# Attention items by feature tile and query tile instead of by head, with one weight pair moved

## The chip, the cores and the metric

The kernel runs on one core of one Trainium2 chip. The metric is the device time of one execution in microseconds (us), as the median of several runs.

## What is computed

Two blocks run one after the other on 256 tokens of 1024 features: a first block (a mixer and a mixture of experts) and a second block of two layers (l = 0 and 1), each with a feed-forward network, an attention part and another feed-forward network. The change is in the attention part of the second block. Cut to what matters there (16 heads of 64 features; 6 window heads with a sink, 4 global heads, 6 neighbourhood heads with a bias; every head sees 256 tokens and 256 context tokens as keys):

```python
p = u @ w_in[l]
q_w, q_g, q_n = _split_q(p[..., :MIX_WIDTH_2])
k_w, v_w, k_g, v_g, k_n, v_n = _split_kv(p[..., MIX_WIDTH_2:])
...
y_w = _window_attn(q_w, k_w, v_w, ck_w, cv_w, sink_win[l])
y_g = _global_attn(q_g, k_g, v_g, ck_g, cv_g)
y_n = _neighbourhood_attn(q_n, k_n, v_n, ck_n, cv_n, rpb_nbr[l])
h = h + gm * (jnp.concatenate([y_w, y_g, y_n], axis=-1) @ w_out[l])
if not last:
    yc = jnp.concatenate([_ctx_attn(cq_w, ck_w, cv_w, sink_win[l]),
                          _ctx_attn(cq_g, ck_g, cv_g),
                          _ctx_attn(cq_n, ck_n, cv_n)], axis=-1)
    hc = hc + cgm * (yc @ w_out[l])
```

where each of these is softmax(q k^T / 8 + bias or mask) v over both kinds of keys.

## The kernel before

Activations lie as [128 features, block, 512 columns]: columns 0 to 255 (X in the code) are the tokens, 256 to 511 (C) the context. All large products run on TensorE (PE) with each operand split into a high and a low part (H and L), so every product is three matmuls. `mm` (line 352) makes the products of one weight tile (a "unit"). Before a unit can run, its raw weights are loaded by SP's queue into one of the tiles `raw`, ScalarE (ACT) casts the high part (`emit_hi`, line 257) and VectorE (DVE) subtracts the low part (`emit_lo`), into a pair of tiles from the list `hls`. That list holds four pairs of its own; other pairs are lent to it for a limited part of the program, from pools that are open then (`extra`) or from attention tiles that are not yet, or no longer, in use (in `mix`, `pt` and two pairs out of the value tiles).

The order of the work is set when the program is built. Main work (units) is emitted in turn; every 3000 columns `work` calls `tick`, which lets background generators take one step each. The attention is such a generator: `attention` is a pipeline over items, and in each step it emits, for the items p1, p2 and p3 of the steps before,

- `t_out(p2)`: the transposed probabilities go from PSUM to the tiles ptH (ACT, line 701) and ptL (DVE),
- `exps(p1)` (ACT, line 908) and `sums(p1)`: exponentials, the reciprocal of their sums (DVE), and the scaling of the first half of the probabilities by DVE and of the second by ACT (line 927),
- `scores` of the new item (PE, line 872) and `maxes` (DVE, which for items with a mask or bias also adds the tile `bias`; then `bias_load` loads the next bias by POOL's queue),
- `v_out(p3)`, `values(p2)` (PE, line 974), `transposes(p1)` (PE, line 942).

Each `yield` hands back to the main program. While units are there, a unit's matmuls (line 352, or line 830 for the values' projections) fill in between; I call this fill. Where the main program has nothing to run before the attention is through (`until` and `drain` in `mix`), the steps follow each other without fill.

A feature tile of 128 rows holds two heads of 64 features. Of items of kind "x" (tokens as queries) there are 16 in each layer, one for each head: i is the feature tile, r the head in it, so that all six score matmuls of an item (64 x 128 weights, 512 columns) read the rows of one half, 64 r to 64 r + 63, three for each of the two query tiles of 128 tokens. Its values are 12 matmuls of 256 columns. Items of kind "c" (context as queries, layer 0 alone, 8 of them) take both heads at once: twelve score matmuls of 256 columns, whose rows alternate between the two halves, and twelve value matmuls. After the attention, `us` holds the output projection: four units over the first five blocks of the features (they are the fill of the last items), then, after `drain(att)`, four over the last three blocks and four over all eight.

Of the kernel before, what the change touches and what calls it, by code (L numbers as in the profile page):

```python
# [32 lines left out]
FR, FH = 8, 0  # L33
# [34 lines left out]
class Free:  # L68
    """Tiles handed out in turn; some are lent, only to units before a limit."""
# [46 lines left out]


class Vector:
    """The vector engine, with a count of the time that its work takes."""
# [14 lines left out]
class Unit:  # L134
    """One weight tile's product: out += W^T rhs over nk blocks of the contraction."""
# [6 lines left out]
class Program:  # L142
# [37 lines left out]
    def warm(self, n):  # L180
        """Keeps the tensor engine's clock up over a wait: products that nobody reads."""
# [26 lines left out]
    def plan(self, mains, adas=(), at=lambda t: t, lead=0, rest=12):  # L208
        """Units in the order of their use, the ones of w_ada spread between the others."""
# [78 lines left out]
    def fill(self):  # L288
        """The parts of a fixed number of weight tiles ahead, and the modulations due by now."""
# [32 lines left out]
    def get_raw(self):  # L322
        """The next of the tiles that are used as they come."""
# [9 lines left out]
    def w(self, i, c):  # L333
        """The parts of a weight tile: the columns a to b of its block k of c."""
# [6 lines left out]
    def mm(self, u, cols, ks=None, start=True, stop=True, parts="HhL"):  # L341
        """parts: H and L are the weight's parts by the activation's first, h the first by its second."""
# [21 lines left out]
    def run_lead(self, us, cols):  # L364
        """Units whose products with the activation's first part go ahead of the others."""
# [37 lines left out]
    def rsqrt(self, ssq, n, scale, parts=None):  # L403
        """rs = (scale * ssq + eps)^-1/2."""
# [15 lines left out]
    def square_in(self, k, cols, src=None):  # L420
        """ssq += src^2, the running sum over the blocks of features; the last square waits."""
# [34 lines left out]
    def norm(self, cols, A, B=None, slow=False):  # L456
        """u = h * rs * A + B into the two parts of u; slowly, between other work, and with few banks."""
# [25 lines left out]
    def scaled(self, cols, A, B, bc, slow=0):  # L483
        """u = h * A * bc + B in two parts; the first part runs ahead of the second."""
# [51 lines left out]
    def ada_next(self):  # L536
        """One block of a modulation vector, for both streams: the rows of w_ada^T by silu(c)."""
# [24 lines left out]
    def silu_c(self, pool, limit):  # L562
        """silu of the two vectors that the modulations come from."""
# [24 lines left out]
    def swiglu(self, f, end):  # L588
        """Epilogues of a gate and an up unit: hid[f] = silu(gate) * up, in two parts."""
# [117 lines left out]
    def rope_tail(self, raw, H, L):  # L707
        """H + L = raw * cos + rot(raw) * sin; raw is [128, 256] of SBUF."""
# [104 lines left out]
    def v_units(self, name, ws, c0, width, per):  # L813
        """Values, token by token: v[:, tile, c0:c0 + width] = u^T W."""
# [29 lines left out]
    def bias_load(self, src):  # L844
        for j in range(2):
            self.nc.gpsimd.dma_start(self.bias[:, j, X], src[:, j, :])

    def attention(self, l, items):
        """Pipelined over the heads: each step has the scores of one, the transposes of the one
        before and the values of the one before that."""  # L850
# [6 lines left out]
        def scores(it):  # L857
            kind, i, r = it["k"], it["i"], it["r"]
# [16 lines left out]
        def maxes(it):  # L875
            """The maxima over the keys, with their sign turned."""
            kind, i, r = it["k"], it["i"], it["r"]
# [5 lines left out]
            for j in range(2):  # L883
# [3 lines left out]
                if it["masked"]:  # L887
                    self.v.tensor_tensor_reduce(out=pj, in0=sj, in1=self.bias[:, j, :], scale=-1.0,
# [1326 lines left out]
```

## Time and profile before

| | |
|---|---|
| median of 3 runs | 2054.43 us (2053.01 to 2055.33) |
| span of the profiled execution, first to last instruction | 2051.0 us |
| time of the profiled execution, by the median | 2054.43 us, so 3.4 us lie around the span |
| busy share of the span: PE, PE weight loads, DVE, ACT, POOL | 98%, 86%, 69%, 41%, 3% |
| the chain of waits that ended last, share of the span by engine | PE 80%, DVE 2%, ACT 2%; by line PE L352 70%, PE L872 2%, PE L974 2%, PE L942 2% |
| attention of layer 0, from the first scores to the end of the last values | 726.9 to 900.5 us |
| attention of layer 1 | 1705.7 to 1825.2 us |

The profile follows one execution. A matmul's duration in it includes the way through the array, so that matmuls overlap; what one costs is read from the distance of starts, or from the chain of waits, which counts each stretch of time once.

### The profile page before, as it was taken

What the parts mean: (1) busy time and instruction counts of PE and PEld (TensorE: products, weight loads), DVE (VectorE), ACT (ScalarE), POOL (GpSimd) and SP (SyncE); (2) the same over time, 40 slices, a digit from 0 to 9 for tenths busy, and PEclk for the clock granted to TensorE, in tenths of its full rate; (3) what the DMA queues carried; (4) which work ended last, traced back from release to release, by engine and by line L of the source; (5) the groups of instructions that cost most, each with busy time, mean ns of one, the idle gap of its engine ahead of it and who ended that gap; (6) DMA issues with size and microseconds to landing.
All of it is one profiled execution on the core that took longest, in us unless ns stands there. A gap on an engine that the chain in (4) does not pass through costs nothing.

```text
span 2051.0 us, 29852 instructions
## 1 busy us (share of the span) xinstructions
PE 2003.9 (98%) x11780; PEld 1757.0 (86%) x11780; DVE 1417.3 (69%) x2368; ACT 838.7 (41%) x1428; POOL 65.3 (3%) x87
## 2 busy tenths in 40 slices
PE   7989989999999999999999999999999999999998
PEld 7977769888888988789888888988888899889998
DVE  6888886888863756777886745788674366767554
ACT  5457653222222456764322222422222245655442
POOL 1200000000000100000000000000000011000000
PEclk9999999999999999999999999999999999999999
DMA  6669973565540311135655533366553122147551
GB/s 235 202 240 362 360 262 123 182 206 197 188 130 22 109 58 39 37 98 179 216 200 176 166 113 113 117 202 195 167 172 108 57 85 74 47 130 240 180 172 44
DMA packets 92596, 318.08 MB, mean 155 GB/s; under 512 B 11616, under 2 KB 14976, under 8 KB 92064
## 3 DMA queue, kind: packets, MB, share of 16 engines
q1 hardware_dynamic: 88496, 306.75, 45.2%
q0 software_dynamic: 2624, 9.08, 1.3%
q8 instruction: 94, 1.54, 0.3%
q14 instruction: 54, 0.44, 0.1%
q10 hardware_dynamic: 1328, 0.27, 0.1%
HBM read 315.01 MB, written 1.05 MB: 154 GB/s over the span
## 4 chain that ended last, share of the span: by engine, by line
PE 80%; DVE 2%; ACT 2%; issue 0%; DMA 0%; POOL 0%; POOLq 0%; DVEq 0%; ACTq 0%
PE bank L352 70%; PE bank L830 3%; PE bank L872 2%; PE bank L974 2%; PE bank L942 2%; DVE tmp L130 1%; ACT probs L908 1%; ACT ptH L701 0%; PE bank L453 0%; DVE uL L130 0%; DVE lo L130 0%; PE bank L449 0%; PE bank L796 0%; DMA raw<-in_w_ffn_up_dram 0%; DVE h L130 0%
## 5 line engine op out<-in xcount | busy, mean ns | idle before, releaser
L352 PE MATMUL bank<-uH,hi 128*128 128x512 f32 (+2 forms) x1128 | 384.1, 345 | 7.1 <-DVEq L1707 6.0
L352 PE MATMUL bank<-uH,lo 128*128 128x512 f32 (+2 forms) x1128 | 380.1, 341 | 0.6 <-DVE lo L130 0.6
L352 PE MATMUL bank<-uL,hi 128*128 128x512 f32 (+2 forms) x1128 | 364.8, 341 | 0.0
L130 DVE CUSTOM_DVE_ANT_0 tmp<-xraw,cs,vec 128x1024 bf16<-128x1024 f32 x192 | 245.9, 1282 | 3.4
L352 PEld LDWEIGHTS bank<-uH,hi 128*128 128x128 f32 x1128 | 217.6, 193 | 33.0 <-DVEq L1707 6.4
L352 PEld LDWEIGHTS bank<-uH,lo 128*128 128x128 f32 x1128 | 217.4, 193 | 23.7 <-DVE lo L130 0.8
L352 PEld LDWEIGHTS bank<-uL,hi 128*128 128x128 f32 x1128 | 207.9, 192 | 21.9
L352 PE MATMUL bank<-uH,xlo 128*128 128x512 f32 (+1 forms) x600 | 201.7, 338 | 0.0
L352 PE MATMUL bank<-uH,xhi 128*128 128x512 f32 (+1 forms) x600 | 201.7, 338 | 0.0
L130 DVE TENSOR_TENSOR lo<-xraw,hi 128x1024 fp32r<-128x1024 f32 (+1 forms) x138 | 164.6, 1200 | 50.6 <-ACT hi L257 50.2
L352 PE MATMUL bank<-uL,xhi 128*128 128x512 f32 (+1 forms) x600 | 198.1, 338 | 0.0
L604 ACT CAST hidH<-tmp 128x512 fp32r<-128x512 f32 (+1 forms) x97 | 51.6, 532 | 331.4 <-DVE tmp L130 331.3
L257 ACT CAST hi<-xraw 128x1024 fp32r<-128x1024 f32 (+1 forms) x138 | 141.1, 1030 | 102.9 <-PE bank L352 91.8
L130 DVE TENSOR_TENSOR lo<-raw,hi 128x1024 fp32r<-128x1024 f32 (+3 forms) x129 | 144.2, 1123 | 46.3 <-ACT hi L257 46.1
L130 DVE SCALAR_TENSOR_TENSOR h<-bank,modT,h 128x256 f32<-128x256 f32 x204 | 92.8, 480 | 112.1 <-PE bank L352 112.1
L352 PE MATMUL bank<-hidH,hi 128*128 128x256 f32 (+1 forms) x504 | 169.8, 337 | 0.0
L352 PE MATMUL bank<-hidL,hi 128*128 128x256 f32 (+1 forms) x504 | 169.1, 335 | 0.1
L352 PE MATMUL bank<-hidH,lo 128*128 128x256 f32 (+1 forms) x504 | 169.0, 335 | 0.0
L257 ACT CAST hi<-raw 128x1024 fp32r<-128x1024 f32 (+3 forms) x129 | 124.3, 968 | 60.8 <-PE bank L352 40.3
L595 ACT ACTIVATE tmp<-bank 128x512 f32<-128x512 f32 (+1 forms) x97 | 49.5, 510 | 232.3 <-PE bank L352 230.5
L130 DVE TENSOR_TENSOR tmp<-tmp,bank 128x512 f32<-128x512 f32 (+1 forms) x97 | 56.0, 577 | 122.9 <-PE bank L352 122.0
L130 DVE CUSTOM_DVE_ANT_0 tmp<-raw,cs,vec 128x1024 bf16<-128x1024 f32 x96 | 123.5, 1287 | 5.7 <-DVEq L1707 3.9
(408 smaller groups left out, 4227.9 us busy)
## 6 DMA issues: line engine op xcount, KB each, us to landing
xraw<-in_w_ada_dram SPq DMA_DIRECT2D x96, 512.0 KB, 3.4
xraw<-in_w_ffn_gate_dram SPq DMA_DIRECT2D x51, 512.0 KB, 3.4
xraw<-in_w_ffn_up_dram SPq DMA_DIRECT2D x51, 512.0 KB, 3.7
raw<-in_w_ada_dram SPq DMA_DIRECT2D x48, 512.0 KB, 4.3
xraw<-in_w_expert_gu_dram SPq DMA_DIRECT2D x43, 512.0 KB, 5.7
raw<-in_w_ffn_up_dram SPq DMA_DIRECT2D x37, 512.0 KB, 3.8
raw<-in_w_ffn_gate_dram SPq DMA_DIRECT2D x37, 512.0 KB, 4.3
xraw<-in_w_ffn_down_dram SPq DMA_DIRECT2D x32, 512.0 KB, 4.0
```

The lines of the kernel that those rows point to most:

```text
L130: return f(*args, **kw)
L257: self.nc.scalar.copy(hi, form(self.raw_of[i][0][:, :n], hi))
L352: nc.tensor.matmul(o, a(k), b[:, k, cols], start=start and k == ks[0] and j == 0, stop=stop and k == ks[-1] and j == len(prods) - 1, skip_ ...
L595: nc.scalar.activation(t[:, :cols.stop - cols.start], u.bank[:, cols], AF.Silu)
L604: nc.scalar.copy(H, tt)
L830: nc.tensor.matmul(b, x[:, kk, tok], y(k), start=first, stop=a == ws - 1 and k == per - 1 and j == 2, skip_group_check=True)
L872: nc.tensor.matmul(it["S"][j][:, o], a[rows, i, q], b[rows, kt, kk], start=n == 0 and o.start == 0, stop=n == 2, skip_group_check=True)
L908: nc.scalar.activation(it["P"][:, j, o], src[:, o], AF.Exp, scale=-1.0 if it["masked"] else 1.0, bias=st[:, c:c + 1], accum_out=st[:, 4 + ...
L942: nc.tensor.transpose(b[:, o * P:(o + 1) * P], src, self.ident)
L974: nc.tensor.matmul(b[:n, X], a[:, k + dk, v0:v0 + n], p[:, k, :], start=j == 0 and k == ks[0], stop=j == 2 and k == ks[-1], skip_group_che ...
```

## The change

An x item is now a feature tile and a query tile t (0 or 1) and holds both heads of the feature tile. Its six score matmuls are of the same shapes, but alternate between the rows 0 to 63 and 64 to 127. The transposed probabilities of the two heads go to two pairs `pts` instead of one pair `pt`, 128 columns (one query tile) at a time; so the values of a feature tile, 24 matmuls, are emitted together behind the second query tile, where 12 were behind each head. The bias is loaded for two heads and one query tile at a time, as two loads of the same size. Beside the second pair, `hls` keeps three pairs of its own instead of four. In the pools around the mixes a fifth pair is lent instead (in the first block's pool one instead of none, in the next one instead of none), and in the mixes' own ends four pairs instead of three; what is one less is the number of pairs while the attention runs. The change also drops comments.

```diff
-FR, FH = 8, 0
+FR, FH = 8, 1
...
-            kind, i, r = it["k"], it["i"], it["r"]
+            kind, i, t = it["k"], it["i"], it["t"]
...
             if kind == "x":
-                subs = [[(j, slice(0, 512), slice(j * P, (j + 1) * P), XC, r)] for j in range(2)]
+                subs = [(slice(0, 512), slice(t * P, (t + 1) * P), XC)]
             else:
-                subs = [[(j, slice(256 * a, 256 * a + 256), slice(256 + a * P, 256 + (a + 1) * P), C, j)
-                         for j in range(2)] for a in range(2)]
-            for sub in subs:
+                subs = [(slice(256 * a, 256 * a + 256), slice(256 + a * P, 256 + (a + 1) * P), C) for a in range(2)]
+            for o, q, kk in subs:
                 for n, (a, b) in enumerate(((self.hidH, self.kH), (self.hidH, self.kL), (self.hidL, self.kH))):
-                    for j, o, q, kk, rr in sub:
-                        rows = slice(64 * rr, 64 * rr + 64)
+                    for j in range(2):
+                        rows = slice(64 * j, 64 * j + 64)
...
         def values(it):
-            PH, PL = (t.rearrange("p (k q) -> p k q", q=256) for t in self.pt)
             if it["k"] == "x":
-                subs = [(r, range(4), 0)]
+                subs = [(1, range(4), 0), (0, range(4), 0)]
...
-            if p2:
+            if p2 and p2["t"] == 1:
                 yield from values(p2)
                 yield
...
-                for r in (1, 0):
-                    it = dict(k="x", i=i, r=r, need=need(i))
+                for t in range(2):
+                    it = dict(k="x", i=i, t=t, need=need(i))
...
-            self.hls = Free([(t(f"hi{i}", [P, 1024], F32R), t(f"lo{i}", [P, 1024], F32R)) for i in range(4)])
+            self.hls = Free([(t(f"hi{i}", [P, 1024], F32R), t(f"lo{i}", [P, 1024], F32R)) for i in range(3)])
...
-            def extra(fx, limit, n=4, hl=4):
+            def extra(fx, limit, n=4, hl=5):
...
-                    self.pt = (t("ptH", [P, 1024], F32R), t("ptL", [P, 1024], F32R))
+                    self.pts = [(t(f"ptH{j}", [P, 1024], F32R), t(f"ptL{j}", [P, 1024], F32R)) for j in range(2)]
...
-                extra(self.b1, limit0, n=2, hl=0)
+                extra(self.b1, limit0, n=2, hl=1)
```

How the order of instructions moves is shown at three places. In the rows, numbers behind a name are those of a buffer. First PE, layer 0, the score matmuls of one x item in the stretch without fill; the two banks are the two query tiles before, the two heads now. Before:

```order
L872 MATMUL bank_65<-kH,hidH 128x512
L872 MATMUL bank_65<-kL,hidH 128x512
L872 MATMUL bank_65<-kH,hidL 128x512
L872 MATMUL bank_69<-kH,hidH 128x512
L872 MATMUL bank_69<-kL,hidH 128x512
L872 MATMUL bank_69<-kH,hidL 128x512
```

Now:

```order
L873 MATMUL bank_67<-kH,hidH 128x512
L873 MATMUL bank_63<-kH,hidH 128x512
L873 MATMUL bank_67<-kL,hidH 128x512
L873 MATMUL bank_63<-kL,hidH 128x512
L873 MATMUL bank_67<-kH,hidL 128x512
L873 MATMUL bank_63<-kH,hidL 128x512
```

The same six matmuls now change bank, and with it the half of the rows, at each one.

Second PE, layer 1, in the stretch without fill: one step of the pipeline before (scores, twelve values, transposes).

```order
L872 MATMUL bank_69<-kH,hidH 128x512
L872 MATMUL bank_69<-kL,hidH 128x512
L872 MATMUL bank_69<-kH,hidL 128x512
L974 MATMUL bank_63<-ptH,vH 128x256 x4
L974 MATMUL bank_63<-ptH,vL 128x256 x4
L974 MATMUL bank_63<-ptL,vH 128x256 x4
L942 MATMUL bank_67<-ident,probs_13147 128x128 x4
L942 MATMUL bank_68<-ident,probs_13147 128x128 x4
```

Now, from the end of one item's scores to the end of the next one's, and on to the values:

```order
L873 MATMUL bank_66<-kH,hidL 128x512
L944 MATMUL bank_70<-ident,probs_13153 128x128 x4
L944 MATMUL bank_67<-ident,probs_13153 128x128 x4
L873 MATMUL bank_65<-kH,hidH 128x512
L873 MATMUL bank_63<-kH,hidH 128x512
L873 MATMUL bank_65<-kL,hidH 128x512
L873 MATMUL bank_63<-kL,hidH 128x512
L873 MATMUL bank_65<-kH,hidL 128x512
L873 MATMUL bank_63<-kH,hidL 128x512
L974 MATMUL bank_69<-ptH_13156,vH 128x256 x4
L974 MATMUL bank_69<-ptH_13156,vL 128x256 x4
L974 MATMUL bank_69<-ptL_13157,vH 128x256 x4
```

One step has no values at all, the next has 24 (the twelve shown, and twelve from the other pair behind them). Steps of the two kinds take turns.

Third ACT, at the end of layer 1's attention: the last copies of transposes and values, then squares of the new h (L426, L429) and the casts of the weights of the output projection (L257; `ptH` and `vH` serve as weight tiles there). Before:

```order
L701 CAST hidH<-bank_67 128x256
L426 ACTIVATE ssq<-h 128x256
L257 CAST ptH<-raw_86 128x1024
L429 ACTIVATE tmp_97<-h 128x256
L257 CAST vH<-raw_87 128x1024
L429 ACTIVATE tmp_99<-h 128x256
```

Now:

```order
L701 CAST hidH<-bank_66 128x256
L426 ACTIVATE ssq<-h 128x256
L257 CAST ptH_13154<-raw_85 128x384
L429 ACTIVATE tmp_95<-h 128x256
L257 CAST ptH_13156<-raw_86 128x1024
L429 ACTIVATE tmp_97<-h 128x256
```

Four of the units after the attention have 384 columns of weights. All four of them were cast before the attention ended; now the last of the four is cast behind it, and the ones of 1024 columns one place later.

## Rows read from the trace of the kernel before

**Rows 1.** The page, part 1: TensorE's busy time, share of the span, instructions.

```profile
PE 2003.9 (98%) x11780; PEld 1757.0 (86%) x11780; DVE 1417.3 (69%) x2368; ACT 838.7 (41%) x1428; POOL 65.3 (3%) x87
```

**Rows 2.** Windows over both attentions: stretch, length, busy us, clock, DMA.

```profile
core 0: us, PE busy (x) PEld busy (x) DVE busy (x) ACT busy (x) POOL busy (x), PEclk, DMA share, GB/s
726.90:822.30 95.40, 94.60 (x577) 79.37 (x576) 58.10 (x134) 55.08 (x145) 7.49 (x5) 1.00 0.15 48
822.30:854.10 31.80, 30.79 (x213) 25.19 (x213) 25.66 (x57) 26.63 (x69) 2.14 (x4) 1.00 0.08 24
854.10:880.00 25.90, 25.90 (x140) 20.67 (x139) 16.00 (x40) 11.90 (x28) 3.22 (x6) 1.00 0.27 79
880.00:900.50 20.50, 16.94 (x138) 13.83 (x137) 15.25 (x34) 16.76 (x49) 0.00 (x0) 1.00 0.08 27
1705.70:1775.60 69.90, 69.90 (x473) 62.68 (x472) 47.62 (x109) 42.23 (x98) 6.54 (x5) 1.00 0.22 65
1775.60:1798.80 23.20, 23.20 (x149) 19.00 (x149) 18.41 (x41) 17.95 (x41) 2.15 (x4) 1.00 0.13 36
1798.80:1825.20 26.40, 24.72 (x180) 21.75 (x179) 18.54 (x45) 16.68 (x38) 3.22 (x6) 1.00 0.31 98
```

**Rows 3.** The chain in order of time: start, us, what it waited through, instructions.

```profile
804.57 0.90 PE bank L872 x12
...
808.48 1.39 PE bank L352 x6
809.87 0.87 PE bank L942 x8
...
830.54 1.59 PE bank L872 x6
...
1721.13 1.44 PE bank L352 x12
```

**Rows 4.** Timeline of PE without fill, layer 0: start, us, what, idle before.

```profile
827.98 0.74 PE L974 MATMUL bank<-ptH,vH 128*128 128x256 f32 x4
...
829.50 1.04 PE L942 MATMUL bank<-ident,probs 128*128 128x128 f32 x8
...
832.06 0.68 PE L974 MATMUL bank<-ptH,vH 128*64 128x256 f32 x4
...
833.49 1.03 PE L942 MATMUL bank<-ident,probs 128*128 128x128 f32 x8
...
837.32 1.09 PE L942 MATMUL bank<-ident,probs 128*128 128x128 f32 x8 [0.27 <-DVE probs L130]
...
841.58 1.14 PE L942 MATMUL bank<-ident,probs 128*128 128x128 f32 x8 [0.72 <-DVE probs L130]
...
880.04 1.03 PE L942 MATMUL bank<-ident,probs 128*128 128x128 f32 x8
...
883.94 1.09 PE L942 MATMUL bank<-ident,probs 128*128 128x128 f32 x8 [0.34 <-DVE probs L130]
```

**Rows 5.** Timeline of ACT behind the transposes at 829.50.

```profile
830.14 1.07 ACT L701 CAST ptH<-bank 128x512 fp32r<-128x512 f32 x2 [0.43 <-PE bank L942]
...
832.80 0.73 ACT L927 ACTIVATE probs<-probs,sm 128x512 f32<-128x512 f32 x1 [0.23 <-DVE sm L130]
```

**Rows 6.** Timelines at the end of layer 1's attention: PE, ACT, DVE.

```profile
1825.22 0.28 PE L352 MATMUL bank<-hidH,hi 128*128 128x256 f32 x1
...
1827.69 1.03 ACT L257 CAST ptH<-raw 128x1024 fp32r<-128x1024 f32 x1
...
1828.75 1.23 DVE L130 TENSOR_TENSOR ptL<-raw,ptH 128x1024 fp32r<-128x1024 f32 x1 [0.35 <-ACT ptH L257]
```

**Rows 7.** Windows at a low and at the full granted clock.

```profile
1848.00:1850.00 2.00, 2.00 (x11) 2.00 (x10) 2.00 (x6) 2.00 (x7) 0.00 (x0) 0.50 0.72 287
1852.00:1854.00 2.00, 2.00 (x19) 2.00 (x18) 2.00 (x4) 1.98 (x2) 0.00 (x0) 1.00 0.00 0
890.00:901.00 11.00, 8.52 (x59) 6.60 (x57) 7.20 (x17) 8.67 (x30) 0.00 (x0) 1.00 0.01 1
```

More of the change, by code (lines that the diff above doesn't have):

```diff
@@ L842, in v_units, with bias_load @@
         self.have.add(name)
-    def bias_load(self, src):
-        for j in range(2):
-            self.nc.gpsimd.dma_start(self.bias[:, j, X], src[:, j, :])
+    def bias_load(self, srcs):
+        for j, src in enumerate(srcs):
+            self.nc.gpsimd.dma_start(self.bias[:, j, X], src)
     def attention(self, l, items):
@@ L875, in maxes @@
         def maxes(it):
-            kind, i, r = it["k"], it["i"], it["r"]
+            kind, i = it["k"], it["i"]
             it["P"] = self.probs.get()
@@ L887, in maxes @@
                 if it["masked"]:
-                    self.v.tensor_tensor_reduce(out=pj, in0=sj, in1=self.bias[:, j, :], scale=-1.0,
+                    bias = self.bias[:, it["t"] if i < 3 else j, :]
+                    self.v.tensor_tensor_reduce(out=pj, in0=sj, in1=bias, scale=-1.0,
                                                    scalar=nsk if it["sink"] else 3.0e38, op0=OP.add, op1=OP.min,
@@ L898, in head @@
         def head(it, j):
-            return 6 * l + it["i"] + 3 * (it["r"] if it["k"] == "x" else j)
+            return 6 * l + it["i"] + 3 * j
         def exps(it):
@@ L957, in values @@
         def values(it):
-            i, r = it["i"], it["r"]
+            i = it["i"]
             v0 = 0 if i < 3 else 128 if i < 5 else 256 + 128 * (i - 5)
-            PH, PL = (t.rearrange("p (k q) -> p k q", q=256) for t in self.pt)
             if it["k"] == "x":
-                subs = [(r, range(4), 0)]
+                subs = [(1, range(4), 0), (0, range(4), 0)]
             else:
                 subs = [(1, range(2, 4), 0), (0, range(2), 2)]
-            if it["k"] == "c" or r == 1:
-                self.vbank = yield from self.take(self.banks)
-            b = it["V"] = self.vbank
+            b = it["V"] = yield from self.take(self.banks)
             for rr, ks, dk in subs:
                 n = 64 * (rr + 1)
+                PH, PL = (t.rearrange("p (k q) -> p k q", q=256) for t in self.pts[rr if it["k"] == "x" else 0])
                 for j, (a, p) in enumerate(((self.vH, PH), (self.vL, PH), (self.vH, PL))):
@@ L1001, in attention @@
                 maxes(it)
-                if it.get("next") is not None:
+                if "next" in it:
                     self.bias_load(it["next"])
                 yield
-            if p3 and (p3["k"] == "c" or p3["r"] == 0):
+            if p3 and p3["t"] == 1:
                 v_out(p3)
-            if p2:
+            if p2 and p2["t"] == 1:
                 yield from values(p2)
@@ L1020, in att_items @@
             for i in grp:
-                for r in (1, 0):
-                    it = dict(k="x", i=i, r=r, need=need(i))
-                    n = 2 * (i - 5) + 1 - r
-                    if i == 2 and r == 0:
-                        it["next"] = self.I["bias"][l, 1]
-                    elif 0 <= n < 5:
-                        it["next"] = self.I["bias"][l, (n + 1) ^ 1]
+                for t in range(2):
+                    it = dict(k="x", i=i, t=t, need=need(i))
+                    n = 2 * (i - 5) + t if i > 4 else -1 if (i, t) == (2, 1) else 9
+                    if n < 5:
+                        a, nt = (n + 1) // 2, (n + 1) % 2
+                        it["next"] = [self.I["bias"][l, 2 * a + r, :, nt, :] for r in range(2)]
                     out.append(it)
@@ L1030, in att_items @@
                 for i in grp:
-                    out.append(dict(k="c", i=i, r=0, need=need(i)))
+                    out.append(dict(k="c", i=i, t=1, need=need(i)))
         return out
@@ L1037, in mix @@
         self.have = set()
-        self.bias_load(self.I["mask"])
+        self.bias_load([self.I["mask"][:, j, :] for j in range(2)])
         def qk(i):
@@ L1078, in mix @@
         f = lambda v: v.rearrange("p a c -> p (a c)")
-        self.hls.lend([self.pt] + [(f(self.vH)[:, 1024 * a:1024 * a + 1024], f(self.vL)[:, 1024 * a:1024 * a + 1024])
-                                   for a in range(2)], self.mix_end[l])
+        self.hls.lend(self.pts + [(f(self.vH)[:, 1024 * a:1024 * a + 1024], f(self.vL)[:, 1024 * a:1024 * a + 1024])
+                                  for a in range(2)], self.mix_end[l])
         if both:
```

8 lines of the change are left out of this document (4 added, 4 removed).

## The prediction

> **What bounds the kernel now.** Read the page first: PE is busy 98% of the span [rows 1], so time is won where PE's work gets shorter, and only there. Then the windows over the two attentions [rows 2]: seven stretches, 293 of 2051 us, cut where fill (matmuls of units between the steps) begins and ends. Stretches 1, 3 and 5 have fill; 2 and 6 have none, 4 none, and 7 has fill for its first half. In 1, 3, 5 and 6 PE hardly idles; in 2 and 4 it idles 1.0 and 3.6 us. Then the chain in order of time, for what a group costs on PE [rows 3]: six score matmuls of an x item take 1.59 us, twelve of half the columns in a c item, which alternate between the halves of the rows, 0.90. Both stream 3072 columns. That pair of rows is the price of the first part of the change, read before it is made. Last the timelines where there is no fill [rows 4, 5], for what a step costs when PE is not the bound.
>
> There, a step runs from transposes to transposes. At 829.50 to 833.49 PE takes 3.99 us: transposes 0.87, scores 1.59, values from 832.06 to 833.49 1.43, and 0.10 between groups [rows 3, 4]. But right behind it, where the scores were the cheap kind, the step from 833.49 to 837.32 took 3.83 and PE sat idle 0.27 before its transposes [rows 4]. That is a second chain, through other engines: ACT begins to copy 0.64 us after the transposes begin, copies for about 1 us, makes the exponentials, and DVE and ACT scale at 3.30 [rows 5]; half a microsecond later the next transposes may start. This chain has 3.83 us for an x item without a mask, 3.90 for one with a bias (880.04 to 883.94) and 4.26 for a c item (837.32 to 841.58) [rows 4]. It is just hidden now: 3.99 against 3.83. Scores are not in it.
>
> **The change part by part.** *Scores.* I price an x item's scores at 0.90 instead of 1.59, 0.69 less. Bounds: no overlap (1.59) and the c row (0.90); I take the c row, since shapes of 64 rows, banks and alternation are the same, and only the columns per matmul differ. 32 items would give 22 us.
>
> *Values.* Their 24 matmuls cost 1.52 (827.98 to 829.50) and 1.43 [rows 4] as before, 2.95. But steps now come in two kinds: A without values, B with all 24. With fill that is nothing. Without fill, A has 0.87 + 0.90 = 1.8 us of PE work and takes the chain's 3.83; B has 0.87 + 0.90 + 2.95 + 0.10 = 4.8, above the chain. A pair then costs 8.6 where two steps cost 8.0: the cheap scores gain nothing there, and the uneven values lose 0.6. An A step also has one yield less, so three pieces of fill where there were four; the attention runs ahead of its fill a little, which the sums below take from the order of PE's instructions.
>
> *Layer 0* [rows 2]. Stretch 1 (95.4): up to the last fill there are now eight x scores instead of seven, 12 more value matmuls and 3 fewer of fill (half of 1.39 [rows 3]): 8 x 0.90 - 7 x 1.59 + 1.42 - 0.69 = -3.2. Stretch 2 (31.8): the steps are now A, B, A, B and three with no or twelve values, which the chain sets: 3.83 + 4.8 + 3.83 + 4.8 + 4.26 + 3.90 + 3.90, and 0.87 to the fill: 30.2, so -1.6. Stretch 3 (25.9): three scores at -0.69, 12 more values, one group of transposes less: -2.07 + 1.42 - 0.87 = -1.5. Stretch 4 (20.5): only c items are scored; one B step of 4.8 takes the place of 4.26: +0.5. Together -5.8.
>
> *Layer 1.* Stretch 5 (69.9): seven scores -4.8, 12 more values +1.4, 9 fewer fill matmuls (9/12 of 1.44 [rows 3]) -1.1: -4.5. Stretch 6 (23.2): scores and the rest of the fill 2.0, then A, B, A, B and one A with a bias: 2.0 + 3.83 + 4.8 + 3.83 + 4.8 + 3.90 + 0.87 = 24.0, so +0.8. Stretch 7 (26.4): until the fill ends, 9.6 us up to the transposes (24 + 12 + 12 fill matmuls at 0.12, scores 0.90, values 2.95); then A with a bias 3.9, B 4.8, and the last transposes 3.9 later; 1.7 for their copies (0.64 + 1.07 [rows 5]) and 2.95 for the last values: 26.9, so +0.5. Together -3.2.
>
> *One pair less.* While units of 24 matmuls run, a freed pair is refilled in a cast of 1.03 and a subtraction of 1.23 [rows 6] while two others are used up: hidden, at no cost; without that cover 2.3 a unit. At the end of layer 1's attention it is not: the three pairs hold units of nine matmuls of 0.12, 1.08 us each. The fourth is cast behind the first square, which ends 2.47 us after the fill begins (1825.22, 1827.69 [rows 6]), and with both parts at 3/8 of the rows' durations is there at 3.4 at the earliest instead of 3.24; the fifth then at 3.4 + 1.03 + 1.23 = 5.7, where PE wants it at 4.5. About 1.3 us, with bounds 0 (DVE and ACT find a gap) and 3.5 (the raw load behind it, whose tile is freed later, is late too, and the norm's small DVE step now stands behind a subtraction that waits for that load). Layer 0's units there have twice the columns: nothing.
>
> *Bias loads, pools.* Same number, size and queue for the bias, one load each per head and step; its tile is freed after the maxima as before. In the pools the pairs lent grow by the one that the list lost. I cost both at 0; the cover is the main work around them. Without it, a pair that comes free late at a change of pools would cost up to 2.3 us, a cast and a subtraction; one that is free early wins nothing, since PE doesn't wait now.
>
> **Sum:** -5.8 - 3.2 + 1.3 = -7.7. The durations are those of one execution of span 2051.0, 3.4 below the median of 2054.43; the part around the span stays. 2054.43 - 7.7 = 2046.7; I say **2047**.
>
> **Rivals.** *1, everything is won:* PE sets the unfilled steps too, as it does now in stretch 6. 32 x 0.69 = 22 less: 2032.4. For it: no idle time of PE in stretch 6; against: the step of 3.83 with cheap scores, where PE did wait [rows 4]. With half of it, 13 less, 2041.
>
> *2, the chain binds beside fill as well:* a filled A step has 0.87 + 0.90 + 3 x 1.39 = 5.9 us on PE against 3.83 plus a weight cast of 1.03 and the copies of q and k on the same ACT. If half of the 19 filled scores' gain goes so, 6.5 of it is lost: 2053. Against: ACT and DVE are busy 58% to 68% in stretches 1 and 5 [rows 2]. The Trainium skill, "TensorEngine Tiling (Array Packing)", PSUM Bottleneck, speaks for it: packing speeds up the matmuls, not the copies out of PSUM, which may then be the bottleneck. By that rule alone the scores would gain nothing anywhere; the unfilled steps agree with it, the filled ones of stretches 1 and 5 so far do not.
>
> *3, slower, by the clock:* PE would idle about 2 us in every A step without fill. At the end of layer 1, where PE has only the norm's few small matmuls and waits for other engines between them, the granted clock fell to 0.50 (1.2 instead of 2.4 GHz), and then 11 matmuls started in 2 us instead of 19 [rows 7]. If it fell in stretches 2, 6 and 7, their five B steps would go from 4.8 to 4.8 x 19/11 = 8.3, and 2047 would become 2047 + 17.5 = 2064.5; two such steps turn the sign. Against: at 890 to 901 PE idles 2.5 of 11 us, and the clock is 1.00 [rows 7].
>
> *4, the scores don't overlap at 512 columns:* the price stays 1.59. Then the gain of the 19 filled scores (13.1) is gone, and four B steps and the unfilled scores at the head of stretch 6 cost 0.69 more each: 2046.7 + 13.1 + 3.5 = 2063.3.
>
> **How the numbers follow.** A measurement tells 0.2%, 4.1 us, from no change. Forecast (4 to 11 us less) 0.58; rival 1, all or half, 0.10; rival 2 and other losses of the weights that leave 0 to 4 us, 0.21; rival 3 0.05; rival 4 0.06. So faster 0.68, same 0.21, slower 0.11. The range, 8 in 10: from rival 1's half, 2041, to rival 2 with the end of layer 1 at 3.5 instead of 1.3, 2055. It leaves out most of rival 1 and all of 3 and 4.
>
> **What would show it.** Chain: x scores at 0.9 instead of 1.59. Timeline without fill: transposes 3.8 and 4.8 apart in turn, and PE idle 2 us before every second group, waiting for DVE or ACT on the probabilities. Stretch 1 near 92, stretch 5 near 65.5, stretches 6 and 7 no shorter. At the end of layer 1, a wait of PE for a subtraction behind the fourth unit. I am wrong if the unfilled steps all take 3.4 (rival 1), if PE waits for ACT inside the filled stretches (rival 2), if the clock falls below 1.00 there (rival 3), or if the scores stay at 1.6 (rival 4).

## The result, and the profile after

The change made the kernel slower: 2069.94 us (median of 4 runs, 2069.21 to 2073.69) against 2054.44 in runs on the same chip, ratio 1.0083, 95% interval 1.0070 to 1.0095. The forecast was 2047 with a range of 2041 to 2055; it missed by 23 us, on the other side of zero. The profiled execution after has a span of 2067.5 us, 16.5 more than before.

PE's part of the page says that it worked less and waited more. It is busy 7.3 us less than before [rows 1], in a span that is 16.5 longer:

```profile
PE 1996.6 (97%) x11780; PEld 1749.6 (85%) x11780; DVE 1415.4 (68%) x2368; ACT 838.6 (41%) x1428; POOL 64.8 (3%) x87
```

The windows over the same seven stretches, columns as in [rows 2], put the loss in the attentions: 308.1 us instead of 293.1, so 15.0 of the 16.5.

```profile
728.00:826.20 98.20, 95.10 (x594) 78.70 (x594) 60.43 (x140) 56.17 (x148) 6.92 (x5) 0.98 0.15 48
826.20:861.80 35.60, 27.61 (x194) 22.45 (x193) 24.48 (x55) 26.30 (x67) 2.32 (x5) 0.90 0.08 21
861.80:886.20 24.40, 24.40 (x144) 19.75 (x143) 15.72 (x40) 11.51 (x26) 3.10 (x6) 1.00 0.26 75
886.20:908.60 22.40, 17.98 (x137) 15.24 (x136) 14.29 (x31) 16.74 (x49) 0.00 (x0) 0.92 0.05 20
1713.90:1784.30 70.40, 67.85 (x478) 60.47 (x477) 46.86 (x108) 42.03 (x97) 6.55 (x5) 0.98 0.21 68
1784.30:1812.30 28.00, 21.49 (x143) 17.41 (x144) 19.84 (x46) 19.24 (x44) 2.43 (x5) 0.88 0.12 33
1812.30:1841.40 29.10, 24.50 (x184) 22.10 (x183) 17.53 (x43) 15.88 (x37) 2.94 (x6) 0.94 0.26 78
```

Two columns are to be read here. Length less busy time is PE's idle time: 29.2 us in all, 7.1 before [rows 2]. And the granted clock is below 1.00 in six stretches, where before it was 1.00 in all seven [rows 2]. Busy time by what is missing of the clock (27.61 x 0.10 in stretch 2, and so on) is what the slow clock costs: 1.9 + 2.8 + 0 + 1.4 + 1.4 + 2.6 + 1.5 = 11.6 us, some 12. This is a rough figure, and rather low: a row's clock is a mean over time in which PE idles too, and in windows of 1 us the sum comes to 13.5. What is left is PE's work at full clock: 267 us, 286 before. The cheaper scores are there, 19 of the 22 us forecast; 22 of idle time and 12 of slow clock take them back and 15 more.

The chain in order of time shows the scores at the price forecast (1.59 before, [rows 3]), and a step without fill that goes another way. Start, us, what:

```profile
728.12 0.90 PE bank L873 x6
...
838.53 0.45 PE bank L944 x4
...
839.01 1.08 ACT ptH L701 x2
840.09 1.35 ACT probs L910 x4
...
841.66 0.50 DVE probs L130
...
842.21 1.09 PE bank L944 x8
843.30 1.58 PE bank L873 x8
844.88 3.81 PE bank L974 x24
848.69 0.45 PE bank L944 x4
```

From 838.5 to 842.2 the chain goes through ACT and DVE, as forecast for a step without values. In the next step PE is the chain, as forecast too, but 24 values take 3.81 instead of 2.95 and the twelve scores of a c item 1.58 (eight of its records in the row) where they took 0.90 [rows 3]. PE's transposes in the timeline of this stretch, and PE's busy time and clock in windows of 2 us over both steps with values:

```profile
826.01 1.03 PE L944 MATMUL bank<-ident,probs 128*128 128x128 f32 x8
832.09 1.12 PE L944 MATMUL bank<-ident,probs 128*128 128x128 f32 x8 [3.44 <-DVE probs L130]
838.37 1.04 PE L944 MATMUL bank<-ident,probs 128*128 128x128 f32 x8
842.21 1.09 PE L944 MATMUL bank<-ident,probs 128*128 128x128 f32 x8 [1.88 <-DVE probs L130]
848.52 1.04 PE L944 MATMUL bank<-ident,probs 128*128 128x128 f32 x8
```

```profile
832.00:834.00 2.00, 1.91 (x12) 0.76 0.16 13
834.00:836.00 2.00, 2.00 (x10) 0.50 0.27 85
836.00:838.00 2.00, 2.00 (x17) 0.89 0.03 8
...
840.00:842.00 2.00, 0.32 (x6) 1.00 0.00 0
842.00:844.00 2.00, 1.79 (x14) 0.82 0.00 0
844.00:846.00 2.00, 2.00 (x15) 0.50 0.00 0
846.00:848.00 2.00, 2.00 (x17) 0.83 0.00 0
```

The step without values takes 3.84 (838.37 to 842.21), as forecast. The step with values takes 6.28 and 6.31 (832.09 to 838.37, 842.21 to 848.52) instead of 4.8: behind each of the two waits (3.44 and 1.88 us) the clock falls to 0.50, 1.2 instead of 2.4 GHz.

### The profile page after: what moved, and what is told of

It is laid out like the page before. It is cut to its first block, busy times and chain, and to the rows that moved or that the text cites. A ratio compares the mean times of both kernels' runs of the same rounds, so it can differ in the third digit from the quotient of the medians.

```text
span 2067.5 us, 29862 instructions
## 1 busy us (share of the span) xinstructions
PE 1996.6 (97%) x11780; PEld 1749.6 (85%) x11780; DVE 1415.4 (68%) x2368; ACT 838.6 (41%) x1428; POOL 64.8 (3%) x87
## 4 chain that ended last, share of the span: by engine, by line
PE 79%; DVE 3%; ACT 3%; issue 0%; POOLq 0%; POOL 0%; DVEq 0%; ACTq 0%
PE bank L352 70%; PE bank L974 3%; PE bank L830 2%; PE bank L944 1%; PE bank L873 1%; ACT probs L910 1%; DVE tmp L130 1%; ACT ptH L701 1%; DVE lo L130 0%; DVE probs L130 0%; DVE ptL L130 0%; DVE sm L130 0%; PE bank L453 0%; PE bank L449 0%; PE bank L796 0%
## 5 line engine op out<-in xcount | busy, mean ns | idle before, releaser
L352 PE MATMUL bank<-uH,hi 128*128 128x512 f32 (+2 forms) x888 | 302.6, 346 | 8.0 <-DVEq L1706 6.5
L352 PE MATMUL bank<-uH,xhi 128*128 128x512 f32 (+2 forms) x832 | 283.3, 342 | 2.1 <-ACT uH L1138 2.1
L352 PE MATMUL bank<-uH,xlo 128*128 128x512 f32 (+2 forms) x832 | 282.1, 341 | 0.0
L352 PE MATMUL bank<-uL,xhi 128*128 128x512 f32 (+2 forms) x832 | 276.9, 340 | 0.0
L352 PEld LDWEIGHTS bank<-uH,xhi 128*128 128x128 f32 x832 | 158.9, 191 | 20.5 <-ACT uH L1138 2.4
L352 PEld LDWEIGHTS bank<-uH,xlo 128*128 128x128 f32 x832 | 158.9, 191 | 17.2
L352 PEld LDWEIGHTS bank<-uL,xhi 128*128 128x128 f32 x832 | 156.0, 191 | 17.1
L130 DVE TENSOR_TENSOR xlo<-xraw,xhi 128x1024 fp32r<-128x1024 f32 (+1 forms) x97 | 115.2, 1188 | 47.2 <-ACT xhi L257 46.8
L352 PE MATMUL bank<-hidH,xhi 128*128 128x512 f32 (+1 forms) x400 | 133.9, 335 | 0.0
L352 PE MATMUL bank<-hidL,xhi 128*128 128x512 f32 (+1 forms) x400 | 133.8, 334 | 0.0
```

Of the source, the lines that this page charges most:

```text
L130: return f(*args, **kw)
L352: nc.tensor.matmul(o, a(k), b[:, k, cols], start=start and k == ks[0] and j == 0, stop=stop and k == ks[-1] and j == len(prods) - 1, skip_ ...
```

## The experiments

Three theories. T1: the uneven steps. Steps without values leave PE idle, and the steps behind them run at the slow clock. T2: the missing weight pair. T3: the chain through ACT and DVE (order of their work, banks), which items of both heads make longer. The table gives for each kernel the median, the ratio to the kernel before in the same runs with its interval, and, from its profile, the length of both attentions, PE's idle time in them and what the slow clock cost (busy time by what is missing of the clock), worked out as above from one window row for each layer, and as rough. The letters are those of the sections below; the prediction's A and B are steps, not these kernels.

| kernel | median us | ratio | length | idle | slow clock |
|---|---|---|---|---|---|
| before | 2054.44 | 1 | 293.1 | 7.1 | 0 |
| the change | 2069.94 | 1.0083 (1.0070 to 1.0095) | 308.1 | 29.2 | 12 |
| A one pair less alone | 2058.86 | 1.0025 (1.0015 to 1.0035) | 294.0 | 7.6 | 0 |
| B uneven values alone, with A | 2079.92 | 1.0127 (1.0110 to 1.0144) | 319.2 | 21.9 | 12 |
| C scores not alternating | 2071.84 | 1.0084 (1.0067 to 1.0101) | 311.6 | 28.7 | 16 |
| D filler of 16 products | 2078.99 | 1.0126 (1.0109 to 1.0143) | 317.4 | 12.9 | 7 |
| D filler of 6 products | 2064.79 | 1.0055 (1.0038 to 1.0072) | 302.8 | 17.1 | 7 |
| E exponentials and scaling first | 2096.05 | 1.0201 (1.0181 to 1.0221) | 333.6 | 43.9 | 25 |
| E exponentials, copies, scaling | 2082.47 | 1.0146 (1.0129 to 1.0163) | 317.5 | 39.6 | 10 |
| F even values, ahead of copies | 2064.94 | 1.0057 (1.0040 to 1.0074) | 302.8 | 28.5 | 9 |
| F with E's second order | 2073.02 | 1.0102 (1.0085 to 1.0119) | 310.9 | 33.9 | 10 |
| G fill in pieces of 2000 | 2067.75 | 1.0076 (1.0059 to 1.0093) | 303.5 | 28.9 | 6 |
| G fill in pieces of 1500 | 2083.75 | 1.0146 (1.0129 to 1.0163) | 308.5 | 27.2 | 12 |
| G seven split output units | 2081.40 | 1.0128 (1.0110 to 1.0146) | 320.6 | 26.2 | 12 |
| H even values, copies apart | 2040.88 | 0.9942 (0.9926 to 0.9959) | 277.6 | 12.2 | 0 |
| H with pieces of 2000 | 2053.61 | 0.9998 (0.9988 to 1.0007) | 290.8 | 20.2 | 3 |

**A. One pair less, alone** (the kernel before with this edit only):

```diff
-FR, FH = 8, 0
+FR, FH = 8, 1
-            self.hls = Free([... for i in range(4)])
+            self.hls = Free([... for i in range(3)])
-            def extra(fx, limit, n=4, hl=4):
+            def extra(fx, limit, n=4, hl=5):
-                extra(self.b1, limit0, n=2, hl=0)
+                extra(self.b1, limit0, n=2, hl=1)
```

> The kernel before with one part of the change alone: three weight pairs in the list instead of four, the fourth lent to the pools; the attention as it was. Theory T1 (the clock falls in the steps with values that follow an idle step) and theory T3 (the steps' chain through ACT and DVE grew longer) leave nothing for the pair: 2054 to 2056 us, with the seven stretches of the attentions as long as before (95.4, 31.8, 25.9, 20.5; 69.9, 23.2, 26.4) within 0.5 each. Theory T2 (the missing pair makes PE wait for casts and subtractions): 2060 to 2070, with new waits of PE for a weight cast or a subtraction. The prediction's own price was 1.3 us at the end of layer 1's attention.

Measured 2058.86, some 5 us more (3 to 7 by the interval), between the two bands. The attentions are as long as before, as T1 and T3 said, and there are new waits for weights, as T2 said. 1.2 us lie ahead of layer 0's attention, where PE waits for a cast and a subtraction, which it never did before; the waits of PE between 660 and 690 us (in total, times, longest):

```profile
PE bank L352 <- DVE lo L130: 0.9, 1, 0.9
PE bank L352 <- ACT hi L257: 0.3, 1, 0.3
```

The changed kernel has the same two rows. Another 1.6 us of waits for a subtraction at 940 to 960 stand in this kernel's trace alone, and a start that took 1.9 us longer, before any weight is used up. At the end of layer 1's attention, where the prediction put 1.3, from the end of the last values to the next network's first product the change took 22.5 us (1841.3 to 1863.9) against 21.9 before (1825.4 to 1847.3): 0.6.

**B. Uneven values, with the scores as they were** (A, and of the attention's change only this):

```diff
-            PH, PL = self.pt
+            PH, PL = self.pts[it["r"]]
-                subs = [(r, range(4), 0)]
+                subs = [(1, range(4), 0), (0, range(4), 0)]
-            if p2:
+            if p2 and p2["r"] == 0:
                 yield from values(p2)
```

> The kernel before with three pairs in the list and, of the attention's change, only the values: a second pair of probability tiles, and the 24 value matmuls of a head pair in every second step instead of 12 in each. Items stay one head by both query tiles, so that the scores keep their 1.59 us. The pair alone gave 2058.9. T1 (uneven steps idle and then run at 1.2 GHz): a step without values has 0.87 + 1.59 = 2.5 us of PE work in a chain of 3.8, so PE idles 1.3 instead of 1.9; where the clock falls behind it the step with values takes 7.2 to 7.5 instead of 5.4: 2075 to 2085. If the clock does not fall behind 1.3 us: 2062 to 2068. If the uneven values cost nothing and the loss comes with the items of both heads (T3): 2059 and then the cheaper scores are what brings the waits.

Measured 2079.92, 21 above A: T1's band. Scores stay at 1.59, so the trace has the whole price of the uneven steps: 14 us of idle time and 12 of slow clock more than A. Its windows over the two attentions:

```profile
727.80:916.40 188.60, 174.75 (x1064) 144.46 (x1064) 115.30 (x265) 110.72 (x289) 12.34 (x15) 0.96 0.13 41
1721.50:1852.10 130.60, 122.52 (x801) 107.03 (x801) 84.81 (x193) 77.05 (x175) 11.99 (x15) 0.96 0.19 61
```

The change is then three steps: A +5, B +21, and items of both heads with cheap scores on top, 2079.9 to 2069.9, -10. These ten are half of what PE's work falls by (285 to 267): in B's uneven steps PE idles already, and shorter scores there make it idle longer (21.9 to 29.2).

**C. Scores that don't alternate** (an x item's three of the first head, then three of the second):

```diff
-                for n, (a, b) in enumerate(...):
-                    for j in range(2):
+                order = [(j, p) for j in range(2) for p in parts]
+                for j, (n, (a, b)) in order:
```

> The changed kernel, but an x item's scores of the first head all go ahead of those of the second, so that they no longer alternate between the halves of the rows; columns, steps and pools stay. Scores go from 0.90 back to about 1.59. If PE sets the filled stretches, 19 filled scores cost 0.69 more each, 13 us: 2083, less what a shorter idle in the steps without values gives back to the clock. T3 (ACT and DVE set the filled stretches as well): the longer scores lie in PE's waits, 2070 to 2073.

No theory was told apart, because the scores did not become dearer. They still cost 0.90, by the chain:

```profile
730.26 0.90 PE bank L875 x6
734.11 0.90 PE bank L875 x6
```

The timeline shows the two heads' matmuls starting in pairs, though the code puts them three and three. So what made them cheap is that one group has both halves of the rows, not that the code alternates them.

**D. Filler in the idle steps**: small products of 128 columns that nobody reads, where the main program waits, so that the clock stays up. First 16, then 6.

```diff
+            elif self.idle and it and self.banks.q:
+                self.warm(WN)
```

> The changed kernel plus 16 small products of 128 columns that nobody reads, put on PE in the steps without values, only where no unit is at hand to fill them. They use PE time in which it idles now (1.9 to 3.4 us a step). T1: the granted clock stays at 1.00 in the steps with values, these go from 6.45 to 4.8 us, and about six of them give back 1.65 each, 10 us: 2058 to 2062. T3: the clock has no part in the end of a step, the steps stay as long: 2068 to 2072. If the time falls by less than 4 us though the clock is 1.00, the rest is in the chain.

> The first filler of this kind made the idle steps 1.85 us longer (32 matmuls, 3.84 us, where PE had 1.9 to idle), and that hid what the clock gives back. Now 6 products instead of 16, 1.44 us, in the same steps: PE has 0.87 + 0.90 + 1.44 = 3.2 us of work in a step of 3.7, so that the step should stay as long. T1 (the clock is 10.5 us of the loss): it stays at 1.00 in the steps with values, these take 4.8 instead of 6.45, 2058 to 2061. T3 (waits on ACT and DVE alone): 2069 to 2072.

Sixteen were too many: 32 matmuls, 3.84 us, where 1.9 were idle. The clock was 1.00 in the steps of stretch 2 and a step with values took 4.78 (832.87 to 837.65), but nine idle steps became longer. With six, 2064.79: 5 us less than the change, half of what T1 said. Its windows over the step with values that took 6.31 above:

```profile
842.00:844.00 2.00, 1.64 (x15) 1.00 0.00 0
844.00:846.00 2.00, 2.00 (x22) 1.00 0.00 0
846.00:848.00 2.00, 2.00 (x20) 1.00 0.00 0
```

It takes 4.84 here (842.83 to 847.67), the 4.8 forecast, and the step without values ahead of it, 3.84 as in the change. Over both attentions the slow clock falls from 12 to 7 us. In the steps of stretches 2 and 6 none is left (1.00 from 826 to 850 and from 1780 to 1812); what stays is in stretch 1, behind the same kind of wait as in the change (0.50 from 784 to 791 us), and at the end of layer 1 (0.50 from 1829 to 1835), where no filler stood or not enough. Both of these are longer than in the change. So the clock is shown as a cause: 5 us come back in this run, of 12 by the trace of the change. It is not the whole loss.

**E. Order on ACT and DVE**: the exponentials ahead of the copies, first with the scaling (2096), then without it.

```diff
-            if p2:
-                t_out(p2)
             if p1:
                 exps(p1)
+            if p2:
+                t_out(p2)
+            if p1:
                 sums(p1)
```

> The changed kernel, but in a step the exponentials and the scaling of an item are issued on ACT and DVE ahead of the copies of the transposes of the item before it, not behind them. T3: the copies (about 1 us of ACT, and a subtraction on DVE) leave the chain from scores to transposes, a step without fill and without values goes from 3.7 us to about 2.7, and the waits of the filled stretches shrink: 2045 to 2060. T1: the idle time in the steps without values shrinks as well (1.9 us to about 1), so the clock should fall less often; if the clock stays at 0.50 in the steps with values, the gain is only that of the steps without values, 10 x 1 us less what the values then wait for the copies. T2: no change, 2070.

> The changed kernel, with ACT's order in a step changed: exponentials of an item first (they need only the maxima made a step earlier), then the copies of the transposes, then the scaling; before, the copies stood ahead of the exponentials, and with the exponentials and the scaling both ahead of the copies the time was 2096, since the values then waited for copies that stood behind a scaling. Here no copy waits for the scaling. T3 (the chain through ACT is what the filled stretches and the idle steps wait for): the exponentials, 1.3 us, leave the chain from transposes to transposes, 3.7 to about 2.6 in an idle step, and PE's waits of 5 us in each of stretches 1 and 5 shrink: 2045 to 2055, with the clock's drops rarer since the idle is 0.8 instead of 1.9. T1 alone (drops stay): 2060. If the copies now come later than before because the maxima do, 2070 to 2080.

Both are worse than the change, so T3 as put here falls: with the values uneven, all copies behind the exponentials cost more than they give back. In the second, ACT waits 0.3 to 0.8 us for DVE's maxima before the exponentials, the copies stand behind that, and values (PE waits 13.2 us for `ptH` in all, 2.2 in the change) and DVE's subtractions come later.

**F. Even values** (12 in every step; the second half at the head of the next step), alone and with E's second order. Besides the lines shown, the second head's transposes and copies come first, and the engines of the scaling are swapped (ACT takes the first half, DVE the second); H has this too:

```diff
-                subs = [(1, range(4), 0), (0, range(4), 0)]
+                subs = [(1, range(4), 0)] if half == 0 else [(0, range(4), 0)]
...
+            if p3 and p3["t"] == 1 and p3["k"] == "x":
+                yield from values(p3, 1)
             if p2:
                 t_out(p2)
```

> The changed kernel, but the 24 value matmuls of a pair of query tiles are split: the second head's 12 where all 24 stood, the first head's 12 at the head of the step behind it. Every step then has 12, as in the kernel before; copies and transposes take the second head first, so that the half that is still read stays. Tells whether the loss is in the uneven steps or in pairing the heads as such. T1: steps without fill have 0.87 + 0.90 + 1.45 = 3.2 us of PE work in a chain of 3.8 to 4.0, PE idles 0.6 to 0.8 instead of 1.9 and then none, the clock stays at 1.00, a pair of steps takes 7.7 to 8.0 instead of 10.1: seven pairs give back 14 to 17 us, 2053 to 2056. T3: the copies wait 0.5 us more for the values ahead of them and the chain grows; 2060 to 2066. T2: no change, 2070.

> Both of the two edits before this: values split evenly, and exponentials ahead of the copies. If T1 and T3 both hold, PE sets the steps without fill as well (0.87 + 0.90 + 1.45 = 3.2 us each against 3.99 in the kernel before), and the 22 us of cheaper scores come through nearly whole: 2034 to 2042, below both kernels. If only one of them holds it is as fast as the better of the two alone.

2064.94: 5 us back, not 14. The values stand between the transposes and the scores now, and one head's copy may not begin before they have read the tile. The chain grew: the step from 839.97 to 844.68 takes 4.71, and PE still idles:

```profile
839.97 1.03 PE L943 MATMUL bank<-ident,probs 128*128 128x128 f32 x8
...
844.68 1.09 PE L943 MATMUL bank<-ident,probs 128*128 128x128 f32 x8 [1.38 <-DVE probs L130]
```

With E's order, 2073: worse than F alone, as that order was worse for the change; neither came near what I had written.

**G. More fill for the idle steps**: smaller pieces (after 2000 or 1500 columns instead of 3000, while the attention runs), or seven split output units instead of four.

```diff
+                self.unit = UM
```

```diff
-NO = (4, 4)
+NO = (7, 7)
```

> The changed kernel, with smaller pieces of fill: while the attention runs, its next part comes after 2000 columns of a unit's products instead of 3000 (0.92 us instead of 1.39). Steps with fill are shorter (4.5 us without values, 8.5 with, against 5.9 and 10.3) and still above the chain of 3.8, so that the attention is further on when the fill ends and fewer steps are left without fill. T1 and T3: each step that moves beside fill gives back its idle time and its share of the slow clock, some 2 us: with two to four steps moved, 2060 to 2066. If the steps are held up by the heads' own projections (an item may not start before its units), nothing moves: 2070. If ACT and DVE cannot follow the shorter steps, waits inside the filled stretches grow: 2072 to 2076.

> As the kernel with pieces of 2000 columns, with 1500 (0.69 us): filled steps of 3.9 us without values, at the chain's 3.8. If the gain of the pieces of 2000 comes from steps moved beside fill, it is larger here, 2054 to 2062; if ACT and DVE cannot follow, PE now waits inside the filled stretches and the time is above that of the pieces of 2000.

> The changed kernel, with seven of the eight output units split into five heads' part and three heads' part instead of four: three more units of 15 matmuls run between the last steps of each layer's attention (stretches 4 and 7), where PE idles and the clock falls. T1 and T3: most of the idle time of stretch 4 (5 us) and of stretch 7 (4 us) is filled, and the clock stays up there (2 to 4 us more): 2058 to 2062. Against it: six more residual additions on DVE (0.48 us or more each), and smaller units at the end of layer 1's attention, where three weight pairs must be refilled every 1.08 us: up to 4 us back, 2062 to 2066.

Pieces of 2000 gave 2 us. With 1500, layer 0's attention was 6 us shorter than the change's (174.6) and layer 1's 6.5 longer (133.9), and some 14 us more went between the two attentions. Seven split units brought 15 us more of work into the attentions, yet idle time and slow clock stayed near the change's (26 and 12), and what follows, which has that work less, became only 3 us shorter between the attentions (802.5 instead of 805.3) and no shorter behind layer 1's. Neither was followed up. No way of spreading the fill came near the kernel before.

**H. Even values behind the scores, copies apart.** Open by now was whether the missing half of the scores' gain goes to the uneven steps or comes with items of both heads. Each step has 12 values, behind the scores; the second head's copies come first, ahead of the exponentials, and the first head's, whose values come a step later, at the end.

```diff
             if p2:
-                t_out(p2)
+                t_out(p2, 1)
             if p1:
                 exps(p1)
                 sums(p1)
...
             if p3 and p3["t"] == 1:
+                if p3["k"] == "x":
+                    yield from values(p3, (0,))
+                    yield
                 v_out(p3)
+            if p2:
+                t_out(p2, 0)
             if p2 and p2["t"] == 1:
-                yield from values(p2)
+                yield from values(p2, (1,) if p2["k"] == "x" else (1, 0))
```

> The changed kernel, with 12 value matmuls in every step and the copies of a step parted: the second head's transposes are made and copied first, ahead of the exponentials; the first head's are copied at the end of the step, behind the scaling, since their values come a step later. The earlier even split put the values ahead of the copies and lengthened the chain (idle 28 us, slow clock 9); here they stand behind the scores. If what the uneven steps cost (idle steps, and the slow clock behind them) is the whole loss, a step without fill has 3.2 us of PE work in a chain shorter by one copy and one subtraction (0.54 and 0.65), 3.2 to 3.7: idle time falls from 29 to 12 us or less, the slow clock from 13.5 to under 3, and the cheap scores come through: 2035 to 2048, below both kernels. If PE's waits come with items of both heads as such (banks, DVE's queue), idle time stays above 22 and the time above 2056.

> The same with pieces of fill of 2000 columns. If the copies apart already leave PE no idle time in the steps without fill, the size of the pieces changes nothing (within 3 us of it); if they still idle there, some 3 us less.

2040.88 us, ratio 0.9942 (0.9926 to 0.9959): 29 below the change and 13 below the kernel before. It has the change's items, its scores, its three pairs, and as much PE work. Its windows over the two attentions, and PE's transposes without fill in layer 0:

```profile
730.20:894.80 164.60, 157.43 (x1064) 130.73 (x1064) 114.55 (x265) 110.80 (x289) 11.37 (x15) 1.00 0.15 47
1699.80:1812.80 113.00, 107.96 (x801) 94.93 (x801) 84.55 (x194) 77.35 (x175) 11.92 (x15) 1.00 0.22 71
```

```profile
828.06 1.09 PE L943 MATMUL bank<-ident,probs 128*128 128x128 f32 x8 [1.41 <-DVE probs L130]
831.60 1.09 PE L943 MATMUL bank<-ident,probs 128*128 128x128 f32 x8
835.01 1.09 PE L943 MATMUL bank<-ident,probs 128*128 128x128 f32 x8
838.98 1.14 PE L943 MATMUL bank<-ident,probs 128*128 128x128 f32 x8 [0.35 <-DVE probs L130]
```

Steps of 3.54, 3.41 and 3.97, little idle time, the clock at 1.00: idle 12.2, slow clock 0, work 265. So items of both heads as such don't make the loss: with even values and less in front of the exponentials it is gone. Since this kernel changes the split, the order of the copies and the engines of the scaling at once, the share of each is not told apart (F, the split in a worse place with the same swap, gave 5; the copies apart with the values left uneven were not run). With pieces of 2000 layer 0 is the same (164.8) and layer 1's attention 13 us longer (126.0), with waits from its first steps on; I expected at most 3 us of difference, and the cause was not followed up.

## Why the prediction was wrong

- **Scores: right.** 0.90 instead of 1.59, and PE's work fell by 19 to 21 us of the 22.
- **The step that failed: values, "B has 0.87 + 0.90 + 2.95 + 0.10 = 4.8".** It was priced at full clock. Measured 6.3 behind an idle step, 4.8 with the filler (D). Rival 3 had the mechanism and its place (the steps with values of stretches 2, 6 and 7; stretch 4 came on top), at 8.3 a step and a chance of 0.05; that its 2064.5 lies near the time measured is luck in part, since a slow step cost 1.5 and not 3.5 more and other losses made up the rest. The sum had put about 2 us of idle time into every step without values and then looked for a fall only at one spot where PE idles 2.5 of 11 us [rows 7], in pieces of under 1 us. That was no evidence on a single wait of 1.9. Of the 12 us of slow clock, 8 lie here (stretches 2, 4, 6 and 7: 2.8 + 1.4 + 2.6 + 1.5); the other 3 are in stretches 1 and 5, behind the waits of the next point. The Trainium skill, "TensorE: Matmul & The Clock Gate", section "HAM oscillation — how this bites in real kernels", describes the like for waits on DMA: each piece of work behind such a wait starts throttled, every time. The trace agrees in part: behind eight of the change's ten waits of 1.88 us and more in the attentions the clock was 0.50, behind two it stayed at 1.00 (last section).
- **Idle time in the filled stretches: missed.** Stretches 1 and 5 idle 3.1 and 2.6 us (0.8 and 0 before). The single waits are 0.34 and 2.17 at 781 to 785, the second for DVE's subtraction of values that holds a bank, and 1.88 at 1724 for the scaled probabilities. Rival 2 had such waits (it ended at 2053); some 5 us, and the slow clock of these stretches comes with them. The wait of 2.17 is not in kernel A; kernel B has it, F with even values too, H has no wait for the probabilities of over 1.5 us and not this one. So it is neither the pair nor the unevenness alone; which order of banks makes it stays open.
- **The chain without fill: right** (3.84 against 3.83), but not for the first step behind fill: 6.08 in layer 0 (826.01 to 832.09), where ACT has the last unit's epilogue and a weight cast ahead of its copies, and 4.57 in layer 1 (1786.27 to 1790.84). That is 3.0 more.
- **By stretch.** Against the lengths of the forecast (92.2, 30.2, 24.4, 21.0; 65.4, 24.0, 26.9) the seven stretches came out 6.0, 5.4, 0, 1.4, 5.0, 4.0 and 2.2 longer, 24.0 in all, nearly the whole miss (24.2 by the spans). The slow clock is 12 of that, new idle time in stretches 1 and 5 is 5, and the first steps behind fill are 3. Some 4 stay unassigned, half of it in stretch 1, where PE's work fell by 1.4 (94.60 to 95.10 - 1.9) and not by 3.2.
- **One pair less: too low.** 1.3 was forecast; alone (A) it cost 5, by the interval 3 to 7. In the change's trace 1.2 + 0.6 show, most of it at another place than forecast, and at the forecast's place PE does wait 0.76 for a subtraction, which it did not before (until 1847.06). Whether it costs the change more than that is not shown.
- **The copies as a limit.** The prediction quoted the Trainium skill, "TensorEngine Tiling (Array Packing)", PSUM Bottleneck: copies out of PSUM may bind. H has the same copies and ends 13 us below the kernel before. So what bound was where the copies and values stood, not the amount of copies.

## What to carry to other kernels

When a change makes work cheaper on the bounding engine, ask what each step then looks like alone: an average step that is long enough does not help if every second one is empty. Price a step that follows an idle one at both levels of the clock, and give that case a real chance as soon as your own sum has PE idle. Where two steps are uneven, moving half of the work by one step, and only the copies that it needs ahead of the exponentials, was worth more here than filler, more fill or another order.

## What was not expected of the hardware

- Two heads' score matmuls on the two halves of the rows overlap when they are issued three and three as well as in turn: 0.90 us for six either way (C), 1.59 when all six are on one half.
- The same wait did not always bring the slow clock. In the change the wait of 1.88 us before 842.21 brought 0.50, those of 1.96 before 860.67 and of 1.97 before 1811.17 did not: the clock stayed at 1.00 from 858 to 866 and from 1808 to 1816. In kernel B the wait of 1.90 before 850.79 us left it at 1.00 too (22 matmuls in the 2 us from 852), and one of 2.76 before 837.16 brought some 10 us at 0.50 (836 to 847). Which waits bring it was not settled.
